# The second output projection of a two-layer backbone step by Strassen's scheme on quarters

## The chip, the cores and the metric

One core of a Trainium2 chip runs the whole step as one program. The metric is the device time of one execution in microseconds (us), the median of several runs. PE is the matrix engine, PEld its weight loads, DVE the vector engine, ACT the scalar engine, POOL GpSimd, SP the engine whose queue issues nearly all transfers (DMAs). Weights lie in HBM, work tiles in SBUF, matmul results in PSUM.

## The reference

Tokens are 512 latent and 128 context ones, T = 640 in all; the width is 2048. Cut to what matters here:

```python
def _odd_mixer(h, w_in, w_out, ...):
    xb, gate = jnp.split(h @ w_in, 2, axis=-1)
    ...                                   # conv, gates, two scans -> y
    return (y * jax.nn.silu(gate)) @ w_out, final

xp = xp + g_p * out_p                     # context tokens
xs = xs + g_s * out_s                     # latent tokens
y_prompt = _rmsnorm(xp, final_norm_g)
y_sample = _rmsnorm(xs, final_norm_g)
```

The change concerns the last `@ w_out` (2048 x 2048, the array `c_out`), the residual with its gate, and the final norm. All is float32.

## The kernel before, in words

Activations lie transposed: channel tile k (128 channels, k = 0 to 15) by 640 tokens. A float32 product is made of three matmuls in the type float32r: each operand is split into a high part and the rest, and high by high, high by low and low by high are added up in PSUM. For the weights ACT casts the high part (`wh`, 128 x 1024: eight 128 x 128 blocks, half of the weights of one output tile) and DVE subtracts it from the raw tile (`wl`). `Stream` does that: `load` issues the DMA of a raw tile, `advance` the cast, `finish` the subtraction and then the next load; there are 3 buffers each of `raw`, `wh` and `wl`.

`project` makes one output tile: for both token halves (320 each) and 16 k it issues three matmuls, 96 in all, into two PSUM accumulators from `r_acc` (three buffers). The second output projection is 16 such tiles. Tile 0 is made at the end of the stage before ("lru", the recurrent mixer), the others in the stage "out1". `mixd1` (profile name `mixe`) holds the mixer's output tiles in HBM; `load_mixed` brings them back while the last gate projection runs, and `split_mixed` makes their high and low parts (`mh`, `ml`; `md` for one that needs no trip).

After each tile `out_project` works on it: DVE adds the residual `xr` to the gated accumulator (`xo`), ACT squares it (`sq`), DVE sums the squares (`sqa`), ACT multiplies by the norm's weight. For the last two tiles the token halves are cut at 384 and `ending` closes the norm of the first 384 tokens while PE still works on the other 256: column sums of `sqa` by PE, a reciprocal root on 3 or 2 columns (`small`), a diagonal matrix `dg` spread by PE, 16 multiplications shared by DVE and POOL, and 8 DMAs of `y`.

The program is straight-line code. A planner writes it at build time: each piece of work is a Python generator, `Clock` keeps an estimated time per engine, and `Order` lets a piece go on when the estimate says that its data is ready. What it decides is the order of instructions on each engine. On the chip every engine runs its list strictly in that order, and so does each issuing queue: an instruction that waits holds up all behind it.

`Clock` puts every transfer on one line at 360 KB per us, whatever its kind:

```python
if op == "dma_start":
    self.t[engine] = at + (0.47 if engine == "Q" else 1.0)
    ...
    begin = max(at + 1.1, self.t["DMA"])
    end = self.t["DMA"] = begin + size / 360e3
```

## Time and profile before

| | |
|---|---|
| median of 3 runs | 2304.67 us (2299.78 to 2307.65) |
| the profiled execution | 2299.91 us, its span 2298.1 us |
| PE, PEld, DVE, ACT, POOL busy | 93%, 88%, 73%, 47%, 37% of the span |
| stage "out1" | from about 2066 us to the end |
| DMA in the steady part of out1 | about 100 GB/s |

Busy time of PE counts a matmul from its start to its modelled end, and neighbours overlap: a 128 x 320 matmul is shown with 0.31 us while a new one starts every 0.147 us. So PE's pace is read from the distance of starts, or from a queue that follows PE, not from the mean of one matmul. Starts in the timeline are us from the span's start. Where a group of rows ends in "12.3 <-PE acc", the engine stood idle for 12.3 us before those instructions and PE's `acc` ended the wait.

### The profile page before, as it was taken

Reading aid. Unit: us, or ns where it says so; the run is one execution under the profiler, and the core shown is the slowest. Engines: PE = TensorE matmul, PEld = TensorE weight load, DVE = VectorE, ACT = ScalarE, POOL = GpSimd, SP = SyncE. Lnnn points to the kernel's source line nnn. Section 1 sums busy time; section 2 is a strip of 40 time slices with the busy share of each in tenths; the row PEclk is TensorE's granted clock in tenths of the full one; section 3 lists DMA queues with packets and bytes.
Section 4 is the critical chain, followed back from the end, with each engine's and each line's share of the span. In section 5 each row is a group of like instructions: output and inputs, shape, how many; then the busy total and the mean of one; then the engine's idle time right before and its main releaser. Section 6 shows DMA issues by size and latency. Waiting matters only on the chain. (4 is left out here: it accounts for less than half of the span.)

```text
span 2298.1 us, 37534 instructions
## 1 busy us (share of the span) xinstructions
PE 2130.1 (93%) x14567; PEld 2025.0 (88%) x14567; DVE 1673.0 (73%) x2560; ACT 1086.3 (47%) x1814; POOL 845.3 (37%) x678
## 2 busy tenths in 40 slices
PE   4899989988989999999998999899999999999997
PEld 1579888877878999999987999799999999999997
DVE  6968775898877888887887676787886667783334
ACT  5555555555553333333353333576565554662222
POOL 3424443445344666566563222444530101110002
PEclk9899999999999999999998999999999999999998
DMA  9864434222225444444455555333322222243223
GB/s 367 301 247 131 136 114 135 84 100 86 93 95 194 140 147 147 140 139 146 148 200 175 191 188 183 98 116 114 117 79 88 85 85 86 80 171 109 97 97 131
DMA packets 127449, 320.62 MB, mean 140 GB/s; under 512 B 14246, under 2 KB 22279, under 8 KB 127272
## 3 DMA queue, kind: packets, MB, share of 16 engines
q1 hardware_dynamic: 125480, 313.20, 40.5%
q0 software_dynamic: 1792, 5.04, 0.7%
q8 instruction: 114, 1.87, 0.3%
q14 instruction: 63, 0.52, 0.1%
HBM read 281.86 MB, written 36.32 MB: 138 GB/s over the span
## 5 line engine op out<-in xcount | busy, mean ns | idle before, releaser
L318 PE MATMUL acc<-h,wh 128*128 128x320 f32 x2544 | 810.0, 318 | 24.9 <-DVE xo L318 9.0
L318 PE MATMUL acc<-h,wl 128*128 128x320 f32 x2544 | 793.0, 312 | 0.0
L318 PE MATMUL acc<-l,wh 128*128 128x320 f32 x2544 | 792.4, 311 | 0.0
L318 POOL TENSOR_TENSOR macc<-macc,mprod 128x512 f32<-128x512 f32 x289 | 434.7, 1504 | 559.2 <-ACT mprod L318 474.1
L318 PEld LDWEIGHTS acc<-h,wh 128*128 128x128 f32 x2544 | 485.2, 191 | 36.0 <-DVE xo L318 9.3
L318 PEld LDWEIGHTS acc<-l,wh 128*128 128x128 f32 x2544 | 484.7, 191 | 0.1
L318 PEld LDWEIGHTS acc<-h,wl 128*128 128x128 f32 x2544 | 483.6, 190 | 0.0
L318 ACT CAST wh<-raw 128x1024 fp32r<-128x1024 f32 x241 | 252.4, 1047 | 413.0 <-PE acc L318 370.0
L318 DVE TENSOR_TENSOR wl<-raw,wh 128x1024 fp32r<-128x1024 f32 x241 | 318.0, 1320 | 171.5 <-ACT wh L318 169.2
L318 PE MATMUL acc<-mh,wh 128*128 128x320 f32 (+2 forms) x1024 | 318.9, 311 | 11.2 <-ACT mh L318 8.8
L318 ACT ACTIVATE mprod<-mraw,vec 128x512 f32<-128x512 f32 x289 | 209.1, 724 | 237.6 <-POOL macc L318 169.5
L318 PE MATMUL acc<-mh,wl 128*128 128x320 f32 (+2 forms) x1024 | 318.3, 311 | 0.0
L318 PE MATMUL acc<-ml,wh 128*128 128x320 f32 (+2 forms) x928 | 288.0, 310 | 2.4 <-DVE ml L318 2.4
L318 DVE SCALAR_TENSOR_TENSOR macc<-mraw,vec,macc 128x512 f32<-128x512 f32 x191 | 186.2, 991 | 100.8 <-DMA mraw<-in_mod_w_dram 77.3
L318 PEld LDWEIGHTS acc<-mh,wh 128*128 128x128 f32 x1024 | 193.2, 189 | 14.6 <-ACT mh L318 9.2
L318 PEld LDWEIGHTS acc<-mh,wl 128*128 128x128 f32 x1024 | 193.6, 189 | 0.0
L318 PEld LDWEIGHTS acc<-ml,wh 128*128 128x128 f32 x928 | 175.1, 189 | 4.1 <-DVE ml L318 3.7
L318 POOL COPY stout<-hs 128x1 f32<-128x1 f32 x32 | 20.5, 639 | 319.2 <-DVE hs L318 319.2
L318 PE MATMUL g<-xhl,wh 128*128 128x322 f32 x512 | 115.7, 314 | 2.2 <-ACT ri L318 2.2
L318 POOL TENSOR_TENSOR y<-y,t 128x256 f32<-128x256 f32 x80 | 84.2, 1072 | 43.0 <-DVE t L318 34.1
L318 POOL TENSOR_TENSOR xo<-xo,sq 128x384 f32<-128x384 f32 (+1 forms) x13 | 11.5, 916 | 239.8 <-ACT sq L318 239.8
L318 DVE SCALAR_TENSOR_TENSOR xo<-acc,modc,xr 128x128 f32<-128x128 f32 (+3 forms) x96 | 38.8, 434 | 82.6 <-PE acc L318 73.7
(303 smaller groups left out, 3369.4 us busy)
## 6 DMA issues: line engine op xcount, KB each, us to landing
mraw<-in_mod_w_dram SPq DMA_DIRECT2D x256, 256.0 KB, 3.3
raw<-in_w_in_dram SPq DMA_DIRECT2D x95, 512.0 KB, 4.0
mraw<-in_mod_w_dram SPq DMA_DIRECT2D x64, 512.0 KB, 7.4
raw<-in_c_in_dram SPq DMA_DIRECT2D x64, 512.0 KB, 3.7
raw<-in_c_out_dram SPq DMA_DIRECT2D x34, 512.0 KB, 3.9
raw<-in_w_out_dram SPq DMA_DIRECT2D x32, 512.0 KB, 4.0
hd<-ef SPq DMA_DIRECT2D x48, 256.0 KB, 3.9
raw<-in_c_gates_dram SPq DMA_DIRECT2D x16, 512.0 KB, 3.5
```

Source lines behind the costliest of these rows:

```text
L318: f(*args, **kw)
```

## The change

The weight matrix W is cut into quarters W11, W12, W21, W22 (output half, then input half), the 2048 channels of the mixer's output into two halves, the tokens into FORE (0 to 319) and REAR (320 to 639). That gives four token quarters: b11 (channels 0 to 1023, FORE), b12 (the same channels, REAR), b21 and b22 (channels 1024 to 2047). One `quarter` is 8 k by 3 matmuls of 320 columns, 24 matmuls into one accumulator. Strassen's scheme, in Winograd's form, needs seven products of quarters where the plain way needs eight; each product has 8 output tiles. Two of the seven use plain weights (`PLAIN`: b11 with W11, b21 with W12), the other five use sums of quarters (`SUMS`: s2, s1, s3, w22, s4 for each output tile j; w22 is a plain weight, but multiplies a sum of tokens).

The sums of tokens (t1, t2, t3, t4) are made by `token_sum` on DVE, POOL and ACT in the first part of out1, from `mixe` tiles that are loaded once more; t3 and t4 go to HBM (`t34d`) and come back (`waiting`) when the tiles that hold b11 and b21 are free. The sums of weights are made by `Pairs`: SP loads a quarter tile of W21 into an SBUF place, and POOL's queue issues a DMA that adds a second one from HBM to it (`accum_op=ALU.add`). For each j there are three loads (W21 twice, W22), four adding DMAs, two sign changes on ACT, and the cast and subtraction for five items. There are six places of 512 KB (`cr`, three of them the old `raw` buffers); s4 is made in the place of s2. Four more PSUM buffers (`more`) are opened, and `bank` takes the free one that has been free for longest. `use` adds the products to the output tiles, `summed` does residual, squares and weight for a half tile of 320 tokens, `normed_out` the norm of FORE and of REAR.

```diff
+PLAIN = [(0, 0), (0, 1), (0, 2), (1, 0), (1, 1)] + [(_n, _j + 3 - _n) for _j in range(5) for _n in (0, 1)] + [(1, 7)]
+SUMS = [(_j, _s) for _j in range(7) for _s in ("s2", "s1", "s3", "w22", "s4")] \
+    + [(7, _s) for _s in ("s2", "s3", "w22", "s1", "s4")]
...
+    def add(self, t, j, q):
+        while self.clock.t["G"] > Ring.order.time:
+            yield 0.2
+        self.G.dma_start(out=t, in_=self.src[j][("w11", "w21", "w22", "w12").index(q)], accum_op=ALU.add)
+        yield
...
+    def sums(self):
+        for j in range(len(self.src)):
+            t = self.raw[j, "s1"] = yield from self.place()
+            self.Q.dma_start(out=t, in_=self.src[j][1])
+            u = self.raw[j, "s2"] = yield from self.place()
+            Ring.order.spawn(self.two(j, t, u))
+            yield 2.0
+            for name in ("s3", "w22"):
+                t = self.raw[j, name] = yield from self.place()
+                self.Q.dma_start(out=t, in_=self.src[j][1 if name == "s3" else 2])
...
+    def two(self, j, t, u):
+        yield
+        yield from self.add(t, j, "w22")
+        self.S.activation(u, t, AF.Identity, scale=-1.0)
+        self.there.add((j, "s1"))
+        yield
+        yield from self.add(u, j, "w11")
+        self.there.add((j, "s2"))
+
+    def three(self, j, t):
+        yield
+        self.S.activation(t, t, AF.Identity, scale=-1.0)
+        yield
+        yield from self.add(t, j, "w11")
+        self.there.add((j, "s3"))
...
+    def work(self, i):
...
+        self.S.copy(wh, t)
+        yield
+        self.V.tensor_sub(wl, t, wh.bitcast(F32))
+        if name == "s2":
+            Ring.order.spawn(self.four(j, t))
+        else:
+            self.places.free(t)
...
+            o = acc[:, 0:HT]
+            od.until(clock.ready([wh[:, k, :], wl[:, k, :], xh, xl], [o] if k == 0 else []))
+            for n, (w_, x) in enumerate(((wh, xh), (wh, xl), (wl, xh))):
+                PE.matmul(o, lhsT=w_[:, k, :], rhs=x, start=(k == n == 0), stop=(k == 7 and n == 2))
...
-        project(parts2, put_later(first_out), lambda k: od.drain(lambda: parts2[k] is not None))
+        for j in range(3):
+            sums_[j] = r_acc.get()
+            quarter(ws, "b11", sums_[j])
         od.drain()
...
+            S.copy(h22, b22)
+            yield
+            V.tensor_sub(l22, b22, h22.bitcast(F32))
+            V.tensor_sub(b22, b22, b12)
+            yield
+            G.tensor_sub(b12, b12, b11)
+            G.tensor_add(b11, b11, b22)
+            yield
+            S.activation(h2, b11, AF.Identity, scale=-1.0)
+            S.copy(h1, b12)
+            G.tensor_sub(b21, b21, b11)
+            yield
+            V.scalar_tensor_tensor(l2, b11, -1.0, h2.bitcast(F32), op0=ALU.mult, op1=ALU.subtract)
+            V.tensor_sub(l1, b12, h1.bitcast(F32))
...
+        def bank():
+            od.drain(lambda: r_acc.open() or r_more.open())
+            first = lambda r: min([r.over(i) for i, t in enumerate(r.held) if t is None], default=1e9)
+            owner = min((r_acc, r_more), key=first)
...
+            if name == "w12":
+                yield from add(j, "p1", (j, 0), c, acc, True, "c11", True)
+            elif name == "s2":
+                yield from add(j, "p1", a, c, acc, True, "u2", False)
+            elif name == "s3":
+                yield from add(j, "u2", b, a, acc, True, "u3", False)
+            elif name == "w22":
+                yield from add(j, "u3", c, b, acc, True, "c21", True)
+            elif name == "s1":
+                yield from add(j, "u3", a, a, acc, False, "u4", False)
+                yield from add(j, "c21", b, b, acc, True, "c22", True)
+            else:
+                yield from add(j, "u4", a, a, acc, True, "c12", True)
...
+        for n, j in PLAIN[3:]:
+            acc = bank()
+            quarter(ws, "b21" if n else "b11", acc, (lambda k: freed.add((n, k))) if j == 7 else None, pr)
+            od.spawn(use(j, "w12", acc) if n else plain_first(j, acc))
+        of = {"s2": "t2", "s1": "t1", "s3": "t3", "s4": "b22", "w22": "t4"}
+        for j, name in SUMS:
+            acc = bank()
+            quarter(pr, of[name], acc, None, pr)
+            od.spawn(use(j, name, acc))
         od.drain()
```

Three places in the order of instructions follow. The first is ACT's list in the steady part of out1. Before, one output tile gives two casts, a square and a weighting:

```order
L318 CAST wh_22740<-raw_22576 128x1024
L318 CAST wh_22798<-raw_22633 128x1024
L318 ACTIVATE sq_22812<-xo10_22677 128x640
L318 ACTIVATE xo10_22677<-xo10_22677,vec_74 128x640
L318 CAST wh_22859<-raw_22696 128x1024
```

In the change one turn of j (here from s2 of j = 6 to w22 of j = 6 and the sign change for s3 of j = 7) reads as follows; `cr_23249` is the place in which s1 of j = 7 is made, `cr_23055`, `cr_23182` and `cr_23214` hold s1, s3 and w22 of j = 6:

```order
L326 ACTIVATE cr_23282<-cr_23249 128x1024
L326 CAST wh_23325<-cr_23055 128x1024
L326 ACTIVATE sq_23343<-xo12_21567 128x320
L326 ACTIVATE xo12_21567<-xo12_21567,vec_74 128x320
L326 ACTIVATE sq_23358<-xo12_21567 128x320
L326 ACTIVATE xo12_21567<-xo12_21567,vec_74 128x320
L326 CAST wh_23370<-cr_23182 128x1024
L326 ACTIVATE sq_23395<-xo4_21563 128x320
L326 ACTIVATE xo4_21563<-xo4_21563,vec_74 128x320
L326 CAST wh_23412<-cr_23214 128x1024
L326 ACTIVATE cr_23376<-cr_23376 128x1024
```

The sign change that reads the sum of j = 7 (first row) now stands ahead of the cast for s1 of j = 6, whose matmuls come a whole turn sooner. The second place is POOL's list in the same stretch. Before, nothing stood there between the mixer's last `hs` and the final multiplications:

```order
L318 TENSOR_TENSOR hs_21198<-hs_21198,hs_21231 128x128
L318 TENSOR_TENSOR xo0_21600<-xo0_21600,sq1_21594 128x384
```

In the change the adding DMAs stand there, 32 in all, here those for s4 of j = 5, s2 and s3 of j = 6, s1 of j = 7, and s4 of j = 6:

```order
L326 DMA cr_22894<-in_c_out_dram 128x1024
L326 DMA cr_23088<-in_c_out_dram 128x1024
L326 DMA cr_23182<-in_c_out_dram 128x1024
L326 DMA cr_23249<-in_c_out_dram 128x1024
L326 DMA cr_23088<-in_c_out_dram 128x1024
```

The third is SP's list at the start of out1. Before, it alternates one residual and two weight tiles:

```order
L318 DMA out_new_s_dram<-stout 128x32
L318 DMA xr<-x1d 128x640 x2
L318 DMA raw<-in_c_out_dram 128x1024 x2
L318 DMA xr<-x1d 128x640
L318 DMA raw<-in_c_out_dram 128x1024 x2
```

In the change the tiles of the mixer are loaded again there, and the first stores of t3 and t4 follow:

```order
L326 DMA out_new_s_dram<-stout 128x32
L326 DMA cr<-in_c_out_dram 128x1024
L326 DMA xr<-x1d 128x320
L326 DMA xo_21561<-mixe_100 128x2x320
L326 DMA xo_21565<-mixe_108 128x2x320
L326 DMA xo_21562<-mixe_101 128x2x320
L326 DMA xo_21566<-mixe_109 128x2x320
L326 DMA raw<-in_c_out_dram 128x1024
L326 DMA xo_21563<-mixe_102 128x2x320
L326 DMA xo_21567<-mixe_110 128x2x320
L326 DMA cr<-in_c_out_dram 128x1024
```

So the weights of the plain products now queue behind the mixer's tiles on SP.

## Rows read from the trace of the kernel before

**Rows 1.** The page: engines over the span, and PE's granted clock in 40 slices.

```profile
PE 2130.1 (93%) x14567; PEld 2025.0 (88%) x14567; DVE 1673.0 (73%) x2560; ACT 1086.3 (47%) x1814; POOL 845.3 (37%) x678
PEclk9899999999999999999998999999999999999998
```

**Rows 2.** Stretches, from:to; us, busy PE PEld DVE ACT POOL, clock, DMA share, GB/s.

```profile
2050.00:2060.00 10.00, 9.00 (x62) 8.73 (x61) 9.34 (x18) 7.80 (x12) 0.00 (x0) 1.00 1.04 409
2085.00:2141.40 56.40, 56.40 (x386) 56.40 (x386) 17.63 (x25) 14.27 (x17) 0.00 (x0) 1.00 0.31 105
```

**Rows 3.** Timeline of SP's queue, steady part: start, us, what.

```profile
2107.12 0.42 SPq L318 DMA_DIRECT2D xr<-x1d  x1
2113.80 7.38 SPq L318 DMA_DIRECT2D raw<-in_c_out_dram  x2
2121.23 0.43 SPq L318 DMA_DIRECT2D xr<-x1d  x1
```

**Rows 4.** Timeline of PE at tile 0, the one wait there in brackets.

```profile
2059.55 0.41 PE L318 MATMUL acc<-ml,wh 128*128 128x320 f32 x1 [1.00 <-DVE ml L318]
```

**Rows 5.** DVE and ACT by shape, 2040 to 2298: busy us, mean ns, idle before.

```profile
L318 DVE TENSOR_TENSOR wl<-raw,wh 128x1024 fp32r<-128x1024 f32 x34 | 42.0, 1234 | 72.9 <-ACT wh L318 72.9
L318 DVE SCALAR_TENSOR_TENSOR xo<-acc,modc,xr 128x320 f32<-128x320 f32 x14 | 7.7, 551 | 45.2 <-PE acc L318 40.4 <-DMA xr<-x1d 4.7
L318 DVE SCALAR_TENSOR_TENSOR xo<-acc,modc,xr 128x128 f32<-128x128 f32 x18 | 6.0, 342 | 2.4 <-PE acc L318 2.4
L318 DVE SCALAR_TENSOR_TENSOR xo<-acc,modc,xr 128x192 f32<-128x192 f32 x14 | 5.8, 417 | 15.9 <-PE acc L318 15.9
L318 DVE TENSOR_TENSOR xo<-xo,acc 128x384 f32<-128x384 f32 x8 | 4.1, 546 | 0.7 <-ACT sq L318 0.7
L318 DVE TENSOR_TENSOR xo<-xo,acc 128x256 f32<-128x256 f32 x11 | 3.7, 412 | 1.8 <-ACT sq L318 1.8
...
L318 ACT CAST wh<-raw 128x1024 fp32r<-128x1024 f32 x34 | 35.7, 1050 | 152.2 <-PE acc L318 149.6 <-issue 2.6
...
L318 ACT ACTIVATE xo<-xo,vec 128x384 f32<-128x384 f32 x2 | 1.2, 618 | 0.1
L318 ACT ACTIVATE sq<-xo 128x384 f32<-128x384 f32 x2 | 1.0, 522 | 7.1 <-DVE xo L318 7.1
```

**Rows 6.** DMA issues: queue, count, KB each, median us to landing; over the span.

```profile
raw<-in_c_out_dram SPq DMA_DIRECT2D x34, 512.0 KB, 3.9
```

**Rows 7.** The same, 690 to 712 us, where the DMA engines are full.

```profile
sig<-in_sig_dram POOLq DMA_DIRECT2D x2, 768.0 KB, 8.3
raw<-in_w_in_dram SPq DMA_DIRECT2D x3, 512.0 KB, 8.2
```

**Rows 8.** The tile `invo`, 512 KB on POOL's queue: its landings.

```profile
DMA to landing us min/median/max: 8.5/10.7/12.9
```

**Rows 9.** Timeline of ACT, one cast in the steady part.

```profile
2111.46 1.05 ACT L318 CAST wh<-raw 128x1024 fp32r<-128x1024 f32 x1 [6.00 <-PE acc L318]
2112.42 0.73 ACT L318 ACTIVATE sq<-xo 128x640 f32<-128x640 f32 x1
```

**Rows 10.** POOL's multiplications at the end, by shape, columns as in group 5.

```profile
L318 POOL TENSOR_TENSOR xo<-xo,sq 128x256 f32<-128x256 f32 x5 | 3.5, 725 | 4.6 <-ACT sq L318 4.6
```

**Rows 11.** The chain that ended last, its end: start, us, what.

```profile
2272.17 9.98 PE acc L318 x80
...
2282.18 1.07 DVE xo L318 x3
...
2288.64 0.42 DVE xo L318
...
2289.39 2.98 DVE xo L318 x9
```

More of the change, by code (lines that the diff above doesn't have):

```diff
@@ L20 @@
 NS = 512
+HT = 320
 GZ = 642
@@ L450, in get, with __init__, empty, over @@
         return t
+class Places(Bank):
+    def __init__(self, stream, places, shape, dtype, name):
+        self.stream, self.places, self.shape, self.dtype, self.name = stream, places, shape, dtype, name
+        self.held = [None] * len(places)
+    def empty(self, i):
+        ws = self.stream
+        return self.held[i] is None and (
+            i >= RAWS or ws.loaded == len(ws.src) and all(n % RAWS != i for n in (*ws.raw, *ws.left))
+        )
+    def over(self, i):
+        p, tag = self.places[i]
+        return self.order.clock.over(p.used[tag][-1], "Q") if p.used.get(tag) else 0.0
+    def open(self, n=1):
+        return sum(self.empty(i) for i in range(len(self.held))) >= n
+    def ready(self, n=1):
+        return sum(self.empty(i) and self.over(i) <= self.order.time for i in range(len(self.held))) >= n
+    def get(self):
+        i = min((i for i in range(len(self.held)) if self.empty(i)), key=self.over)
+        p, tag = self.places[i]
+        t = self.held[i] = p.tile(self.shape, self.dtype, tag=tag, name=self.name, bufs=1)
+        return t
 class Stream:
@@ L2221, in _kernel, with out_project @@
         od.drain()
-    def out_project(op, layer, src, parts, first, keep, finish, xout, sqa, last=None):
-        r_x = Ring(op, [128, T], F32, "xr", 3 if last else 2)
+    def out_project(op, layer, src, parts, first, keep, finish, xout, sqa):
+        r_x = Ring(op, [128, T], F32, "xr", 2)
         r_sq = Ring(op, [128, T], F32, "sq", 1)
-        pairs = []
         def residual(i):
@@ L2264, in then @@
                 xout[i] = o
-            return putter(write, then) if i < 14 or last is None else last(i, write, o, pairs)
+            return putter(write, then)
         for i in range(16):
@@ new lines, in _kernel, with residuals, token_sums @@
+        finals = [x for j in range(8) for x in ((j, 0), (j + 8, 0), (j + 8, 1), (j, 1))]
+        def residuals():
+            for i, h in finals:
+                while not r_x.ready():
+                    yield 0.3
+                x = res[i, h] = r_x.get()
+                Q.dma_start(out=x, in_=x1d[i][:, REAR if h else FORE])
+                yield
+        def token_sums():
+            for k in range(8):
+                m, c = (k % 6, REAR) if k % 6 < 4 else (k % 4 + 2, FORE)
+                y = [pairs[m + 4 * d][:, :, c] for d in range(2)]
+                while not (
+                    k in mixed_done and k + 8 in mixed_done and (k < 6 or k - 6 in made) and clock.ready([mixd1[k], mixd1[k + 8]], y, "Q") <= od.time
+                ):
+                    yield 0.3
+                for d in range(2):
+                    Q.dma_start(out=y[d], in_=mixd1[k + 8 * d].rearrange("p (c t) -> p c t", c=2))
+                yield 0.5
+                od.spawn(token_sum(k, y))
@@ new lines, in _kernel, with waiting @@
+        made = []
+        def waiting(n):
+            for m in range(4):
+                for k in (2 * m, 2 * m + 1):
+                    while not (k in made and {(n, 2 * m), (n, 2 * m + 1)} <= freed and clock.ready([t34d[k]]) <= od.time):
+                        yield 0.3
+                    name = "t4" if n else "t3"
+                    hi, lo = quarter_at(name, k)
+                    Q.dma_start(out=lo.bitcast(F32), in_=t34d[k][:, FORE if n else REAR])
+                    od.spawn(split_waiting((name, k), hi, lo))
@@ new lines, in _kernel, with place, plain_first, add @@
+        owners = {}
+        def place(i, h):
+            return x2[i][:, REAR if h else FORE]
+        def plain_first(j, acc):
+            while j >= 4 and 4 + j // 6 not in made:
+                yield 0.3
+            S.copy(place(j + 8, 0), acc[:, 0:HT])
+            drop(acc)
+            yield
+            done.add((j, "p1"))
+        def add(j, needs, to, of, acc, last, tells, ends):
+            while (j, needs) not in done:
+                yield 0.2
+            V.tensor_add(place(*to), place(*of), acc[:, 0:HT])
+            if last:
+                drop(acc)
+            yield
+            done.add((j, tells))
+            if ends:
+                od.spawn(summed(*to))
```

296 lines of the change are left out of this document (216 added, 80 removed).

## The prediction

> **What bounds the kernel now.** I read the page first: PE is busy 93% of the span and its granted clock is nine tenths of full speed or more in all but three of 40 slices [rows 1]. Then the stretches of the last stage. There PE has no idle time, DVE works 18 us of 56 and ACT 14, and the DMA engines move about 105 GB/s where they reach 409 shortly before [rows 2]. So the projection runs at PE's pace, and everything else has room. That pace is read from SP's queue, which follows PE: residual tiles are asked for at 2107.12 and 2121.23, 14.11 us apart, and between them lie the 96 matmuls of one output tile [rows 3]. That is 0.147 us a matmul, 3.53 us for a quarter product of 24, and 17.64 us for the five products of one j. PE waits once, 1.0 us, at tile 0, for the low part of a mixer tile [rows 4]. After the last matmul the chain runs some 16 us over residual, squares, norm, multiplications and stores [rows 11].
>
> **PE's work.** Before: 16 tiles of 96, 1536 matmuls. After: seven products of eight tiles of 24, 1344. The matmuls keep their shape, so 192 go, at 0.147 us: **-28.2 us**, if PE stays the bound. At the start the first three products need only the first eight mixer tiles, and only their first 320 tokens, so the wait of 1.0 us should go: **-1.0**.
>
> **The other engines in the steady part.** Each turn of j is 17.64 us of PE. DVE has five subtractions of 1.23 us, six additions from PSUM (0.55 at 384 columns, 0.41 at 256, so 0.48 at 320), four half tiles of residual (0.55 in one piece or 0.42 + 0.34 in two) and four sums of squares, which I also take at 0.48: 6.2 + 2.9 + 2.6 + 1.9 = 13.6 us. ACT has five casts and two sign changes of the same size at 1.05 and four pairs of square and weighting, 0.52 and 0.62 at 384 columns, about 1.0 a pair at 320: 11.4 us [rows 5]. Both are below PE, at 77% and 65%. Before, they were at 31% and 25%; the cover is thinner, but no engine becomes the bound by its work alone.
>
> **The adding DMA.** No row shows one, so I call its time from issue on POOL to landing X and bound it. Below: a plain load of the same 512 KB, 3.9 us [rows 6]. Above: the slowest 512 KB on POOL's queue, `invo`, with 12.9 us, when the DMA engines were full and four others had been issued before it [rows 8]. Between them lies `sig`, 768 KB on the same queue, 8.3 us in the same crowd, where plain loads of 512 KB took 8.2 instead of 3.9 [rows 7]. The steady part won't be that full, but an addition has to fetch what it adds to, besides the 512 KB from HBM. I take **X = 6.5 us**, nearer to the plain load than to the crowd. The traffic of a turn, three loads, four additions and four residual halves, is 4.3 MB if an addition counts once, 245 GB/s.
>
> A rule of the Trainium skill speaks against the change here: "Collectives: The Full Stack", section "The bandwidth ceiling: the fold count and why AG ≠ RS ≠ AR", has an addition in the DMA engines read two sources, and so run at half the rate of a copy. By that rule a turn reads 6.4 MB, 364 GB/s, and an addition takes the DMA engines 2.6 us where a copy at 409 GB/s takes 1.3; on the plain load's 3.9 us, with 0.5 for the other queue, that makes an estimate of X = 5.7, and the sum below would be 2284. No row of before can show it.
>
> **Who waits for X.** The place of W22's quarter of j becomes free when it is cast and subtracted, and then takes the load of W21 for s1 of j + 2. POOL's queue adds W22, and ACT makes the sign change that starts s2. In ACT's list this sign change stands ahead of the cast of s1 of j + 1, so ACT stands still until X is over, and behind it stand that cast, three pairs of square and weighting, the cast of s3, and the cast of W22 of j + 1, which closes a ring. Its length: from the start of a cast to the load that it frees, 2111.46 to 2113.80, is 2.34 us [rows 3, 9]; the load 3.9; then X; the sign change, the cast of s1 and the cast of s3 at 0.96 each, which is the distance from a cast to the next instruction [rows 9]; three pairs, 3.0; handovers 0.4. That is 12.5 + X, against 17.64 of PE. Up to X = 5.1 the ring costs nothing. At 6.5 it is 19.0 us, 1.4 more than PE needs, in seven turns 9.5 us. The lead eats a part of that: an item is cast when its product is still two away, 7.05 us, of which 2.4 go to cast and subtraction, so about 4.3 us are spent before PE waits. The other two additions on that path (W11 for s2, W12 for s4) have more than 11 us each. Steady loss: **+5.2** (0 at X = 5.1 to 50 at X = 12.9).
>
> **Where plain products turn into sums.** Before the third product of sums, PE has 15 products, 53 us. In that time SP's queue must bring 8 weight halves (4.2 MB), 16 mixer tiles (5.2), 4 quarters for j = 0 and 1 (2.1), residuals (0.5), store t3 and t4 (2.6) and load t3 back (1.3), and POOL's queue makes four additions (2.1 to 4.2 MB): 18 to 20 MB, 44 to 49 us at 409 GB/s [rows 2]. So the DMA engines are 83 to 93% full where now they are at a quarter, and SP's list is strict: a store of t34d that waits for a sum of tokens holds up the weights behind it. POOL has 24 additions of 0.73 us at 256 columns [rows 10], some 22 us at 320, which fits. I charge one load as late as those in the full stretch, 8.2 instead of 3.9 [rows 6, 7]: **+4** (0 to 13, three of them).
>
> **The end.** Behind the last product stands one more addition from PSUM (0.48). The last half has 320 tokens and not 256: 11 multiplications on DVE at 0.48 instead of 0.41 [rows 5], +0.8; 0.5 MB more of `y` in the last stores at 409 GB/s, +1.3, half of it under the multiplications. DVE's list puts eight multiplications of FORE among the steps of REAR, 3.8 us, where before two stood there, 1.1; I count half of the difference. With 0.1 for the residual that makes 3.4, say **+4** (2 to 6).
>
> **Sum.** -28.2 - 1.0 + 5.2 + 4 + 4 = -16.0 us. Against the profiled execution's 2299.9 that is 2284; its time is the lowest of those shown, 4.8 under the median, so for a median I predict 2304.7 - 16 = **2289 us**.
>
> **Rivals.** (a) All hidden: X is 5 us or less and the queue keeps up. Then -28.2 - 1.0 + 4 = -25, **2279**. For it: a load in the steady part lands after 3.9 us. Against it: the ring leaves nothing over, and the traffic is more than twice today's. (b) The adding DMA becomes the bound and the kernel **slower**. With X at `invo`'s median of 10.7 us the ring is 23.2 us, 5.6 over PE, 39 in seven turns, less 4.3 of lead: -28.2 - 1.0 + 35 + 8 = +14, **2318**; at 12.9 us 2334. It decides from X = 8.8 us, where the ring gives back all that PE saves. For it: POOL's queue has shown 8.5 to 12.9 us for 512 KB; and if an addition took the engines three times a copy's 1.3 us, the four of a turn with the 2.2 MB of plain traffic would fill 21 us of 17.64 by themselves. Against it: that was in a crowd of six. (c) The start of the stage is short of DMA: three loads late, 13 us instead of 4, and ACT's casts behind late tiles hold up the weights' casts. Then -16 + 9 = -7, and with a little more from the same crowd for the first turns about **2300**, no measurable change.
>
> **Chances.** Runs of before lie within 0.35% of each other; 0.3%, 7 us, is about what can be told from no change. The forecast, X of 5.5 to 8 us with a start that costs up to 8, has 0.48 and its own range, 2280 to 2298. (a) 0.17, (b) 0.21, (c) 0.14. Faster: 0.46 of the forecast, all of (a), 0.04 of (c), 0.67. The same, 2298 to 2312: 0.02, 0.05 of (b), 0.09 of (c), 0.16. Slower: 0.16 of (b), 0.01 of (c), 0.17. The range runs from 2275, which holds nearly all of (a), to 2317, which leaves out half of (b): 2275 to 2317.
>
> **What would show it.** PE: starts still 0.147 us apart, 1344 matmuls in the projection. The additions: their landing in the DMA view, 5.5 to 8 us; under 5 is (a), over 8.8 is (b). ACT: in each turn one wait of the sign change for a DMA, some 4 to 6 us, ahead of a cast; PE's waits behind `wl`, about 1 us a turn, and none before the lead is spent, so none for j = 0 and 1. If PE waits for `wl` more than once a turn, or the wait stands at the cast of s2 or s4, the ring is not the one that I drew. At the start: PE waits for weights or token sums between the plain products and s3 of j = 0, about 4 us in all, and DMA near 400 GB/s there. At the end 18 to 22 us from the last matmul of a product to the last store. The prediction fails if the additions are far from 6.5 us, if DVE's list, 77% full and in strict order, holds up the subtractions (PE would wait for `wl` while ACT had cast long before), or if the sums of tokens arrive later than the plain products last.

## The result and the profile after

The changed kernel takes 2326.19 us, median of 6 runs (2324.07 to 2333.84), against 2305.54 of before beside it: ratio 1.0104, 95% interval 1.0089 to 1.012. It is **slower, by 21 us in the medians and 24 by the ratio**; 2289 with a range up to 2317 was predicted.

The page of the changed kernel, its engines and PE's granted clock, against [rows 1]:

```profile
span 2322.3 us, 37713 instructions
...
PE 2119.1 (91%) x14377; PEld 2009.0 (87%) x14377; DVE 1743.9 (75%) x2703; ACT 1141.2 (49%) x1928; POOL 903.6 (39%) x731
...
PEclk9899999999999999999989999899999999998998
```

PE has 190 recorded matmuls less, and only 11 us less busy time in a span that is 24 us longer: it waits, and its granted clock is below nine tenths in 5 slices instead of 3. Stretches of the changed kernel, columns as in [rows 2]: the junction from plain products to sums, then the sums.

```profile
2085.00:2141.40 56.40, 41.07 (x231) 39.03 (x231) 42.62 (x56) 26.97 (x51) 27.15 (x24) 0.83 0.91 283
2150.00:2250.00 100.00, 90.64 (x572) 87.62 (x571) 59.19 (x101) 50.41 (x71) 16.66 (x19) 0.95 0.90 205
```

In the same 56.4 us PE had 386 matmuls before and now has 231. The DMA engines, a third busy before, are at 0.9 to the end of the loads.

To put the loss into stages I read five starts from PE's timeline. The first is a **mark**, a matmul of a gate projection some 70 us ahead of the stage "out1"; the program up to there is the same. Rows of the changed kernel: the mark, the first product with `t2h` (that of s2, the first of the five of each j) of j = 0, 1 and 7, and the last product's end.

```profile
1996.71 0.45 PE L326 MATMUL g<-xhl,wh 128*128 128x322 f32 x2
...
2127.81 0.30 PE L326 MATMUL acc<-t2h,wh 128*128 128x320 f32 x1
...
2155.95 0.31 PE L326 MATMUL more<-t2h,wh 128*128 128x320 f32 x1
...
2281.10 0.31 PE L326 MATMUL acc<-t2h,wh 128*128 128x320 f32 x1
...
2299.80 0.31 PE L326 MATMUL more<-qh,wl 128*128 128x320 f32 x1
```

And of the kernel before, the mark and the last matmul:

```profile
1992.85 0.46 PE L318 MATMUL g<-xhl,wh 128*128 128x322 f32 x2
...
2281.86 0.28 PE L318 MATMUL acc<-mh,wl 128*128 128x256 f32 x1
```

From the mark to the span's end it was 2298.1 - 1992.85 = 305.2 us, of which 16.2 lie behind the last matmul. With 192 matmuls (28.2 us) less, 8 turns of 17.64 us for the sums and the same 16.2, the first product of sums would begin 305.2 - 28.2 - 141.1 - 16.2 = 119.7 us after the mark, or 118.7 without the wait at tile 0. Measured:

| stage | if PE were the bound | changed kernel | lost |
|---|---|---|---|
| mark to first product of sums | 118.7 | 131.1 | 12.4 |
| first turn (j = 0 to 1) | 17.6 | 28.1 | 10.5 |
| six turns (j = 1 to 7) | 105.8 | 125.2, 20.9 each in the mean | 19.4 |
| last j, to its last matmul | 17.6 | 18.7 | 1.1 |
| behind it, to the end | 16.2 | 22.5 | 6.3 |

That is 49.7 lost against 29.2 won, +20.5; mark to end 325.6 against 305.2. The last j takes 18.7 us in e4 and k1 below too, which have no adding DMA.

PE's one long wait in the first turn is for the low part of a token sum, t2, which DVE makes behind low parts of the sums that come back from HBM and of weights; DVE has no gap in the 10 us before. Here the changed kernel's, and that of f1 below, where no addition is made:

```profile
2136.36 0.63 PE L326 MATMUL acc<-t2l,wh 128*128 128x320 f32 x1 [5.41 <-DVE t2l L326]
```

```profile
2125.62 0.64 PE L326 MATMUL acc<-t2l,wh 128*128 128x320 f32 x1 [5.32 <-DVE t2l L326]
```

Where a steady turn goes, from three timelines of the changed kernel. SP's queue, two loads that each take the place of W22's quarter, one turn apart; then POOL's queue, with four adding DMAs; then ACT:

```profile
2186.53 0.33 SPq L326 DMA_DIRECT2D cr<-in_c_out_dram  x1
...
2208.15 0.33 SPq L326 DMA_DIRECT2D cr<-in_c_out_dram  x1
```

```profile
2188.19 0.88 POOL L326 DMA_DIRECT2D cr<-in_c_out_dram  x1 [8.17 <-ACT cr L326]
2192.36 0.88 POOL L326 DMA_DIRECT2D cr<-in_c_out_dram  x1 [3.29 <-DVE xo L326]
2193.40 0.88 POOL L326 DMA_DIRECT2D cr<-in_c_out_dram  x1 [0.17 <-issue]
2200.77 0.88 POOL L326 DMA_DIRECT2D cr<-in_c_out_dram  x1 [6.49 <-ACT cr L326]
```

```profile
2199.42 1.06 ACT L326 ACTIVATE cr<-cr 128x1024 f32<-128x1024 f32 x1 [8.68 <-DMA cr<-in_c_out_dram]
2200.38 1.03 ACT L326 CAST wh<-cr 128x1024 fp32r<-128x1024 f32 x1
...
2203.23 1.03 ACT L326 CAST wh<-cr 128x1024 fp32r<-128x1024 f32 x1
...
2205.59 1.03 ACT L326 CAST wh<-cr 128x1024 fp32r<-128x1024 f32 x1
```

This is the ring of the prediction, step by step. A load starts at 2186.53; the addition to it is issued at 2192.36, 5.8 us on (the view names a DVE instruction as what ended POOL's wait there); ACT's sign change has stood for 8.68 us when that lands, at 2199.42, 7.1 us on; then the casts of s1, s3 and W22 at 2205.59, and 2.6 us later the next load. 21.6 us, against 12.5 + 6.5 = 19.0: the load took 1.9 us more than its 3.9, the addition 0.6 more than its 6.5. The six turns lie between 19.5 and 23.8 us.

### The profile page after: what moved, and what is told of

The parts are those of the page before. It is cut to its first block, busy times and chain, and to the rows that moved or that the text cites. A ratio compares the mean times of both kernels' runs of the same rounds, so it can differ in the third digit from the quotient of the medians.

```text
span 2322.3 us, 37713 instructions
## 1 busy us (share of the span) xinstructions
PE 2119.1 (91%) x14377; PEld 2009.0 (87%) x14377; DVE 1743.9 (75%) x2703; ACT 1141.2 (49%) x1928; POOL 903.6 (39%) x731
## 5 line engine op out<-in xcount | busy, mean ns | idle before, releaser
L326 PE MATMUL acc<-h,wh 128*128 128x320 f32 x2544 | 810.9, 319 | 25.8 <-DVE xo L326 8.2
L326 DVE TENSOR_TENSOR wl<-raw,wh 128x1024 fp32r<-128x1024 f32 x223 | 299.5, 1343 | 111.3 <-ACT wh L326 108.8
L326 ACT CAST wh<-raw 128x1024 fp32r<-128x1024 f32 x223 | 233.4, 1047 | 279.0 <-PE acc L326 226.9
L326 PE MATMUL acc<-mh,wh 128*128 128x320 f32 x512 | 160.5, 313 | 17.4 <-ACT mh L326 13.9
L326 PE MATMUL acc<-mh,wl 128*128 128x320 f32 x512 | 159.6, 312 | 0.0
L326 POOL COPY stout<-hs 128x1 f32<-128x1 f32 x32 | 20.5, 640 | 319.2 <-DVE hs L326 319.2
L326 PE MATMUL acc<-ml,wh 128*128 128x320 f32 x448 | 138.9, 310 | 0.0
L326 PEld LDWEIGHTS acc<-mh,wh 128*128 128x128 f32 x512 | 97.0, 189 | 20.5 <-ACT mh L326 14.5
L326 PEld LDWEIGHTS acc<-mh,wl 128*128 128x128 f32 x512 | 97.3, 190 | 0.0
L326 PEld LDWEIGHTS g<-xhl,wh 128*128 128x128 f32 x512 | 87.0, 191 | 3.2 <-ACT ri L326 3.0
L326 POOL DMA_DIRECT2D cr<-in_c_out_dram x32 | 28.2, 921 | 155.4 <-ACT cr L326 79.3
L326 PEld LDWEIGHTS acc<-ml,wh 128*128 128x128 f32 x448 | 84.8, 189 | 0.0
```

The source lines that it names most:

```text
L326: f(*args, **kw)
```

## The experiments

The table gives the same five starts for every kernel: us from the mark to the first product of sums, the first turn, the mean of the six after it, the last matmul to the end, mark to end, and the ratio to the kernel before with its interval (or the one time). The mark itself lay between 1985.5 and 1997.2 us in these executions, so mark to end compares single profiles better than their times do. It is not exact either: for the kernels from e1 on with several runs, their median less their mark to end lies between 1990 and 1996 us, so a difference of some 3 us between two rows is not told from chance.

One part of it can be taken out. Right behind the mark the rest of the gate projection, the same 96 matmuls of `g` in all of them, took 17.9 to 18.0 us in the changed kernel, the one before, e1, e3, e4, e5, f2, k1 and k2, and 16.8 in the others, with a mean granted clock of 0.76 and 1.00 in the 7 us after its one wait of 2 us. Where rows of the two kinds are compared, 1.1 us are added below to the shorter kind.

| kernel | first sum | turn 1 | turns 2-7 | end | mark to end | ratio or us |
|---|---|---|---|---|---|---|
| changed kernel | 131.1 | 28.1 | 20.9 | 22.5 | 325.6 | 1.0104 |
| e1 | 133.1 | 32.7 | 19.4 | 21.6 | 321.6 | 1.0044 (1.0026-1.0062) |
| e2 | 139.3 | 20.8 | 19.5 | 22.4 | 318.0 | 1.0043 (1.0025-1.0061) |
| e3 | 129.6 | 25.8 | 17.8 | 22.4 | 303.3 | 2296.8 us |
| e4 | 119.7 | 24.3 | 17.6 | 22.8 | 291.2 | 2278.6 us |
| e5 | 126.5 | 21.6 | 23.3 | 22.3 | 328.9 | 2319.4 us |
| e6 | 140.8 | 20.0 | 23.1 | 22.6 | 340.4 | 1.0145 (1.0128-1.0163) |
| e7 | 118.7 | 22.0 | 21.8 | 22.5 | 312.9 | 1.0025 (1.0006-1.0044) |
| e8 | 125.1 | 27.8 | 22.8 | 22.4 | 330.6 | 1.0096 (1.0075-1.0117) |
| f1 | 123.0 | 25.3 | 17.6 | 22.5 | 295.2 | 2291.4 us |
| f2 | 128.7 | 24.2 | 26.5 | 22.3 | 353.0 | 1.0214 (1.0188-1.0241) |
| f3 | 122.7 | 27.3 | 20.9 | 22.4 | 316.4 | 1.0029 (1.0015-1.0044) |
| f4 | 139.4 | 21.4 | 20.2 | 22.1 | 322.9 | 2320.6 us |
| k1 | 128.9 | 24.8 | 17.6 | 22.3 | 300.4 | 0.9961 (0.9947-0.9976) |
| k2 | 129.3 | 27.5 | 18.0 | 22.3 | 305.9 | 0.9985 (0.9973-0.9998) |
| k3 | 127.9 | 24.7 | 17.6 | 21.8 | 298.8 | 0.9956 (0.9939-0.9973) |
| k4 | 122.6 | 21.8 | 17.7 | 21.9 | 291.4 | 0.9936 (0.9919-0.9952) |

### The steady turns: order (A) or full DMA engines (B)

**e1**, the planner books an adding DMA at twice its bytes (in `note`):

```diff
-            size = max(1, out.shape[0]) * self.size(out) * 4
+            size = max(1, out.shape[0]) * self.size(out) * (8 if kw.get("accum_op") is not None else 4)
```

> One number of the planner is changed: it books an adding DMA with twice its bytes, so that it reckons the sums ready later, and ACT's list comes out with the sign change for the sum of j+2 behind the casts of s1 and s3 of j+1 instead of ahead of them. The bytes, the DMAs and the matmuls stay. Theory A (the order ring): in the changed kernel ACT stands at the sign change, which waits for a load (5.8 to 6.0 us) and an adding DMA (6.3) in series, with the casts that TensorE needs behind it; a steady turn is then 21.25 us where the matmuls need 17.64. With the sign change behind the casts the ring is open: steady turn at most 18.5 us, and the total 2303 to 2312 us (2326 less some 7 turns of 2 to 3 us). Theory B (the DMA engines are full): their busy share is 0.89 over the steady turns, 18.9 us of each 21.25, and no order makes it less; the turn stays 20.5 or more and the total 2320 to 2328 us.

**e2**, the same with a seventh place:

```diff
-        spread = op.tile([128, HT], F32, name="spread")
+        spread = dg
...
-            Places(ws, [(wpool, f"raw{i}") for i in range(RAWS)] + [(op, f"cr{i}") for i in range(3)], [128, 8, 128], F32, "cr"),
+            Places(ws, [(wpool, f"raw{i}") for i in range(RAWS)] + [(op, f"cr{i}") for i in range(4)], [128, 8, 128], F32, "cr"),
```

> As the kernel in which the planner books adding DMAs at twice their bytes, and with seven places for the sums of weights instead of six (the seventh takes the room of the tile named spread, which shares dg's). Theory A (order ring): a place more lets the loads of j+2 start one product earlier, so the load and the add in series are covered; steady turn 17.6 to 18.2 us, total 2298 to 2308 us. Theory B (DMA engines full): more places only queue more bytes at the same engines; turn 20.5 or more, total 2318 to 2328 us.

Turns of 19.4 and 19.5 us: neither theory's number, though e1's 2311.9 us lies at the end of A's range; e2's 2312.5 lies between the two. The order, in e2 with a seventh place, gave back 1.4 to 1.5 us of 3.3. In e2 the DMA engines were busy for 92.4 of 100 us (57.3 for POOL's queue, 35.1 for SP's, 2150 to 2250), 18.0 us of a turn of 19.5, which is itself more than PE's 17.64: by that share, an estimate, the transfers alone would hold a turn above PE. What was won in the turns of e2 went partly back before the first sum, 139.3 us.

**e3**, POOL's DMAs overwrite instead of adding (the additions are left out):

```diff
-        self.G.dma_start(out=t, in_=..., accum_op=ALU.add)
+        self.G.dma_start(out=t, in_=...)
```

> The POOL DMAs of the sums overwrite instead of adding, so the sums of weights are left out (each tile holds the last quarter alone); bytes read from DRAM, number of DMAs, waits and ACT's order stay as in the changed kernel. What is left is the price of adding. Both theories: landing of the POOL DMA falls from 6.3 to 4 to 5 us, of the SP loads from 5.8 to 4 to 5 us, DMA busy share in the steady turns from 0.89 to 0.55 to 0.65. Theory A (order ring): 12.5 + (4.5 - 3.9) + 4.5 = 17.6 to 18.5 us a turn. Theory B (engines full): 17.64, PE-bound. Total 2296 to 2306 us by both. If the junction (2066 to 2140) still loses 16 us, its loss is not that of the adds; if the total is below 2300, it is.

Landings on the page of e3, POOL's queue and SP's:

```profile
cr<-in_c_out_dram POOLq DMA_DIRECT2D x32, 512.0 KB, 4.8
cr<-in_c_out_dram SPq DMA_DIRECT2D x24, 512.0 KB, 5.0
```

The ring by the prediction's formula is then 12.5 + (5.0 - 3.9) + 4.8 = 18.4 us. The turns were 17.6 three times, by my reading while the lead lasted, and then 18.0, 17.9 and 18.1: the formula is right to 0.4 us here, with the landings put in that were measured. The time before the first sum hardly moved, and first sum and first turn together still lose 19.1 us of 22.9. The total under 2300, which was to show that the junction's loss is that of the adds, came from the turns.

**f2**, the adding DMAs are made, but the planner books nothing for them:

```diff
-        self.G.dma_start(out=t, in_=..., accum_op=ALU.add)
+        self.G.engine.dma_start(out=t, in_=..., accum_op=ALU.add)
```

> The reverse: the adding DMAs are issued, but the planner books nothing for them, so that ACT's order is that of the kernel without POOL DMAs. Theory O: the first product of sums begins at 119 to 122 us, as there; theory D: at 127 us or more. In the steady part the planner now takes the sums to be ready at once, so the sign changes stand at least as early as in the changed kernel: by the ring 21 us a turn or more, total 2320 to 2335 us; by the DMA engines alone 20 to 21 us, 2318 to 2326 us.

Order matters more than I gave it. A turn takes 26.5 us, with the same transfers, and now the DMA engines have room. The stretch 2150 to 2250 of f2, with DMA share 0.71:

```profile
2150.00:2250.00 100.00, 79.09 (x451) 76.12 (x450) 44.48 (x76) 38.63 (x55) 12.23 (x14) 0.83 0.71 167
```

In this order the first sign change stands one cast earlier, ahead of that of s2 of j + 1, and the other one ahead of the cast of W22, so the ring holds a cast and a sign change more and ACT waits up to 11.3 us at its first step. 19.4, 20.9 and 26.5 us a turn come from the same transfers in three orders. The engines alone can't give that; the ring was named, and the total, 2348 us, is 13 above its range. The planner's bookings move other instructions too, so the one place in ACT's list is not tried by itself.

**f4**, e2 with one more DMA per j that nobody waits for and the planner does not book:

```diff
+            if j > 1:
+                self.Q.engine.dma_start(out=self.spare[j], in_=self.src[j][0])
```

> The kernel with seven places and adds booked twice, and per j from 2 on one DMA more on SP that copies 512 KB from DRAM to a spare tile in DRAM, that nobody waits for and the planner does not book: the order is unchanged, the DMA engines get more to do. Theory B (what is left above 17.64 us in that kernel, whose turns two to seven take 19.5 us in the mean, is the DMA engines being full): the turns that have loads left grow by 1.5 to 3 us, 21 to 22.5 in the mean of turns two to five (now 21.1 in the mean of its first four), total 5 to 15 us more. Theory A (it is order that is left): less than 0.5 us a turn.

Mark to end grew by 4.9 us over six such DMAs, 6.8 in the last turn alone (17.9 to 24.7) while turns two to six did not grow. That is less than B expected and more than A, and little more than the 3 us that are not told from chance. So with the order open the DMA engines are a limit near by, whose share of the remaining 1.8 us I can't separate from order.

### The junction

**e4**, no POOL DMAs at all, and **f1**, booked but not issued (the additions are left out in both):

```diff
-        self.G.dma_start(out=t, in_=..., accum_op=ALU.add)
+        self.clock.note("G", "dma_start", (), dict(out=t, in_=..., accum_op=ALU.add))   # f1 only
```

> The 32 POOL DMAs of the sums are left out altogether (the sums of weights are not made), all else stays. Steady turn 17.64 us by all theories (load 3.9 to 4.5 us and sign change only). What it tells apart is the junction: if the stretch 2066 to 2140 loses its 16 us by the DMA engines, which the adds, the mixer tiles and the remaining plain loads fill together (busy share 0.97 to 1.00 in 2080 to 2120), then less than 8 us are lost here and the total is 2280 to 2292 us; if it loses them by the planner's order and by the trip of the token sums through DRAM (landing median 8.1 us), 12 us or more stay lost and the total is 2293 to 2303 us.

> The adding DMAs are booked by the planner as before but not issued (the additions are left out); TensorE, ACT, VectorE and SP then have the changed kernel's order word for word, only POOL loses its 32 DMAs. In the kernel that leaves them out of the booking too, the first product of sums began 119.7 us after the last 322-column product of the projections before (in the changed kernel 131.1), and the turns after it were 24.3 and then 17.6. Theory O (order: the planner, which books adds, puts instructions that wait ahead of casts in the junction): 127 us or more to the first product of sums here. Theory D (the adds' transfers fill the DMA engines): 119 to 122 us. The steady turns say nothing here (no add to wait for): 17.6 by both.

Without adds a turn is 17.6 us, so the PE term holds. Before the first sum, e4 loses 1.0 us, f1, with the changed kernel's order, 5.4 (4.3 and the 1.1 of the mark), and the changed kernel 12.4: the order costs 4.4 and the adds 7.0. f1 came out 1 us above D's range, 2 with the 1.1, and 3 to 4 below O's; e4's one time, 2278.6, is 1.4 below the range of full DMA engines, with a mark 11 us ahead of the changed kernel's. The first turn stays 7 to 8 us too long without any add, with the wait for `t2l` shown above (2.4 us in e4).

**e7** and **f3**, the four adds of j = 0 left out, unbooked and booked:

```diff
+        if j > 0:
-        self.G.dma_start(out=t, in_=..., accum_op=ALU.add)
+            self.G.dma_start(out=t, in_=..., accum_op=ALU.add)
+        else:
+            self.clock.note("G", "dma_start", (), dict(out=t, in_=..., accum_op=ALU.add))   # f3 only
```

> The changed kernel without the four adding DMAs of j=0 (their additions are left out), which all fall between 2075 and 2131; those of j=1 to 7 stay. Theory D (the DMA engines are full in the junction, and the adds fill them): 2066 to 2140 loses 6 to 9 us instead of 15, as in the kernel without any POOL DMA (5.6), the steady turns stay at 21.2 us, total 2314 to 2319 us. Theory T (the trip to t34d and the copy that waits for it): 13 us or more stay lost, total 2322 to 2328 us.

> Only the four adds of j=0 are booked and not issued (left out); order as in the changed kernel but for two rows. Leaving them out of the booking too brought the first product of sums from 131.1 to 118.7 us and the total 18 us down. Theory O: first product of sums at 127 us or more, total 2320 to 2326 us. Theory D: 118 to 121 us, total 2306 to 2312 us.

Those four cost 7.3 us before the first sum with the order kept (f3: 122.7 and the 1.1), 11.3 with their places in the order too (e7: 118.7 and the 1.1). f3's total, 2307.8, lies in D's range; e7's, 2307.1, lies 7 us under D's and more under T's. So the adds being there make the larger part of the loss. That full DMA engines are the reason is not shown: an add that is left out takes its bytes with it and also the wait for its landing. At a copy's price (e3) 129.6 us were needed, only 1.5 less, though the engines' share from 2085 us to the first sum fell from 0.89 to 0.79. Part of this is the clock: from the end of `g` to the first sum PE stood for 9.5 us in the changed kernel, 6.4 in e3, 4.9 in f1, but in e3 more of the rest ran at the lower clock. The three, length less PE's busy time, columns as in [rows 2]:

```profile
2014.60:2127.80 113.20, 103.72 (x674) 102.53 (x674) 83.49 (x121) 61.99 (x101) 38.52 (x35) 0.94 0.69 223
```

```profile
2009.80:2121.40 111.60, 105.22 (x674) 104.04 (x673) 84.15 (x122) 62.01 (x100) 37.72 (x36) 0.94 0.66 226
```

```profile
2011.20:2117.30 106.10, 101.25 (x674) 100.20 (x673) 83.20 (x121) 61.63 (x100) 36.26 (x32) 0.98 0.67 223
```

**e5**, the trip of the token sums through DRAM left out:

```diff
-            Q.dma_start(out=t34d[k].rearrange("p (c t) -> p c t", c=2), in_=y[1])
...
-                    Q.dma_start(out=lo.bitcast(F32), in_=t34d[k][:, FORE if n else REAR])
+                    Q.dma_start(out=lo.bitcast(F32), in_=mixd1[k + 8][:, FORE if n else REAR])
```

> The trip of the two token sums through DRAM is left out of the changed kernel: no store to t34d, and the products with w22 and s1 take their tokens from the mixer's tiles in DRAM (so these products have other numbers). The adding DMAs, ACT's order and the 16 half loads stay. Theory T (the trip): the junction (2066 to 2140) loses its 17 us because ACT's copy of a plain product into a pair tile waits 13.4 us for the store out of that tile, with the casts of the next weights queued behind the copy; without the store less than 9 us are lost there and the total is 2312 to 2318 us. Theory D (the DMA engines are full there): the copy only stands where the next late transfer would have stopped the engines; at least 12 us stay lost and the total is 2320 us or more.

The wait at which I aimed, in ACT's timeline of the changed kernel, its longest in the junction:

```profile
2116.91 0.75 ACT L326 COPY xo<-acc 128x320 f32<-128x320 f32 x2 [13.39 <-DMA t34d<-xo]
```

Without the store this copy no longer waits, and the first sum of j = 0 comes 4.6 us and that of j = 1 11.1 us sooner. But mark to end is 328.9, no better: the planner's order changed with the edit, and the turns behind grew to 23.3. The one time of 2319.4 looks like a gain, but its mark lay 8 us early. T is right about the wait, and its total (2312 to 2318) did not come.

**e6**, the sums of weights held back; **e8**, POOL's part of the token sums on DVE:

```diff
+        while self.hold():            # e6: pr.hold = lambda: len(made) < 6
+            yield 0.3
...
-            G.tensor_sub(b12, b12, b11)      # e8, and so for the two others
+            V.tensor_sub(b12, b12, b11)
```

> One line holds back all loads and adding DMAs of the sums of weights until the token sums of six of the eight tiles are booked; everything moved is the same work later. Theory D (in the junction the DMA engines are full): 2066 to 2140 loses 8 to 12 us instead of 17, since the mixer's tiles no longer share the engines with four to eight adds; the steady turns stay at 21.2 us, total 2317 to 2322 us. Theory T (the copy that waits for the store to t34d): 15 us or more stay lost, total 2324 to 2330 us. If the first sums then come too late, the loss only moves to 2130 to 2160.

> The three operations of each token sum that POOL makes (24 of 128x320, mean 1.15 and 1.5 us in 2066 to 2140) are made by VectorE; nothing else changes. A third theory on the junction, C: VectorE and POOL slow each other there (wl takes 1.43 us beside POOL's sums instead of 1.22, ql<-xo,qh 0.78 instead of 0.47, t2l 0.82 instead of 0.48), so the sums of tokens come late by that; without it the junction loses 9 to 12 us instead of 15 and the total is 2320 to 2323 us. Theory D (DMA engines full): the sums were waiting for bytes anyway, 14 us or more stay lost, total 2324 to 2328 us.

e6 only moved the loss: PE stood for 18 us before the first sum, and 2334.8 us is above both ranges. e8 brought the first sum to 125.1, and lost it again in turns of 22.8; its ratio is that of the changed kernel, and its 2324.7 us lies in D's range. e5 to e8 also reorder the turns behind, which is why I take the junction's shares from f1 and f3, with e4 for what is left without adds.

### A version without adding DMAs

**k1**: four plain loads per j, and the four sums on DVE. **k2**: s1 and s4 on POOL instead. **k3**: k1, and POOL takes 10 of the first half's 16 last multiplications. **k4**: k3 with all token sums on DVE, as in e8. The remarks behind `#` are no part of the code.

```diff
+            w21 = yield from self.get(j, "w21")      # place() and a load on SP
+            w22 = self.raw[j, "w22"] = yield from self.get(j, "w22")
+            w11 = yield from self.get(j, "w11")
+            t = yield from self.place()
...
+        self.V.tensor_add(t, w21, w22)               # s1; self.G in k2
+        self.V.tensor_sub(w21, w11, w21)             # s3
+        self.V.tensor_sub(w11, w11, t)               # s2
...
+        self.V.tensor_add(self.raw[j, "s4"], self.raw[j, "s4"], t)   # s4, t is s2; self.G in k2
...
-                if k % 3 == 2:                       # k3 and k4
+                if k % 3 == 2 or not h and k % 3 == 1:
```

> The sums of weights are made by VectorE in SBUF instead of by adding DMAs: per j four plain loads (w21, w22, w11, w12) on SP, no POOL DMA and no sign change on ACT, four 128x1024 additions or subtractions on VectorE (1.1 to 1.3 us each, as the subtraction for wl 1.22 us). VectorE: 11 us a turn and 4.9 more, 16 of 17.64; DMA as in the kernel without POOL DMAs and one load more, busy share 0.35 to 0.45. Both theories A and B: turn 17.64 and 2280 to 2290 us, faster than the kernel before by 0.5 to 0.8%. A rival: VectorE at 90% in a strict order delays wl and the evictions, turn 18 to 18.5, 2288 to 2296 us.

> As the kernel with the sums on VectorE, but s1 and s4 on POOL (128x1024, 2.6 to 2.9 us by POOL's 725 ns for 128x256) and s2 and s3 on VectorE. VectorE 13.4 of 17.64 us a turn, POOL 5.6. If POOL and VectorE ran beside each other freely this is the lightest split: 2280 to 2286 us. Rival: both work in SBUF at the same time and slow each other (the subtraction for wl grows from 1.2 towards 1.9 us), and s1, on which s2 waits, comes 1.5 us later: 2286 to 2294 us, no better than the sums on VectorE alone.

> The kernel with the sums of weights on VectorE, and in the last normalisation of the first half POOL takes 10 of the 16 multiplications instead of 5. VectorE did 11 of them (0.4 us each) between the last products' additions, in the chain that ends the program (last matmul to the end: 22 us, before 16). If that chain is bound by VectorE the end shortens by 4 to 5 times 0.4 us: 2288 to 2290 us against 2291. Rival: POOL's ten (0.93 us each) slow VectorE beside them and end too late for the second half's share, so that nothing is gained: 2291 to 2294 us.

> As the kernel with the sums of weights on VectorE and the other split of the last multiplications, and the token sums' three POOL operations on VectorE too. In that kernel VectorE is busy for 19.9 of 20 us in 2100 to 2140, with wl at 1.9 us and the 128x320 operations at 1.15 us beside POOL instead of 1.22 and 0.48. Theory C: 24 operations of 0.48 us cost VectorE 11.5 us and give back 24 times about 0.68, 16 us, and each token sum is ready sooner: the junction loses 7 to 9 us instead of 11.6, total 2285 to 2288 us. Theory D (DMA engines): no change, 2288 to 2292 us.

k1 is faster than before by 0.39%. Its 2291.3 us lies in its rival's 2288 to 2296, but not for the rival's reason, turns of 18 to 18.5: the turns are PE's, and first sum and first turn lose 17.4 us, against 22.9 with the adds. k2 is slower than k1, as its rival said, and 3 us above the rival's range. k3 can't be told from k1; the end shrank by 0.5 us where 1.6 to 2 were hoped for, so the multiplications between the additions are at most a small part of those 6 us. **k4 is the best kernel of the study: 2287.44 us against 2301.16, faster by 0.64%** (0.48 to 0.81). DVE by shape in 2066 to 2140, busy us and mean ns, k1 and then k4:

```profile
L326 DVE TENSOR_TENSOR wl<-raw,wh 128x1024 fp32r<-128x1024 f32 x12 | 15.9, 1335 | 9.2 <-ACT wh L326 9.2
L326 DVE TENSOR_TENSOR ql<-xo,qh 128x320 fp32r<-128x320 f32 x16 | 12.0, 752 | 3.6 <-ACT qh L326 3.6
```

```profile
L326 DVE TENSOR_TENSOR wl<-raw,wh 128x1024 fp32r<-128x1024 f32 x11 | 13.3, 1220 | 7.1 <-ACT wh L326 7.1
...
L326 DVE TENSOR_TENSOR ql<-xo,qh 128x320 fp32r<-128x320 f32 x16 | 7.7, 484 | 2.3 <-ACT qh L326 2.3
```

With POOL out of the way the same DVE instructions are shorter, and k4 comes out 4.7 us under k3, in theory C's range, where e8 gained nothing. Whether it is the shorter instructions of DVE or the sums that no longer take POOL's 1.0 to 1.5 us each was not tried apart. The stretch 2150 to 2250 of k4 shows PE without a gap, DVE at 97%, DMA at 0.45:

```profile
2150.00:2250.00 100.00, 100.00 (x683) 100.00 (x683) 97.00 (x149) 52.51 (x77) 0.00 (x0) 1.00 0.45 144
```

## Why the prediction was wrong

**PE's work, -28.2, and the start, -1.0: right.** Turns are 17.6 us wherever nothing waits (e4, f1, k1), e4 needs 119.7 us to the first sum against 118.7, and the wait at tile 0 is gone: from 2010 us on PE first stands for more than 0.3 us at 2090.8 in the changed kernel.

**X = 6.5: right,** 6.3 in the median. DMA issues of the changed kernel, 2150 to 2250, median us to landing last, and its queues, POOL's first, with packets, MB and share of the 16 engines' time:

```profile
q0 software_dynamic: 2869, 10.44, 59.3%
q1 hardware_dynamic: 4562, 9.92, 30.1%
...
cr<-in_c_out_dram POOLq DMA_DIRECT2D x19, 512.0 KB, 6.3
cr<-in_c_out_dram SPq DMA_DIRECT2D x14, 512.0 KB, 5.7
```

Per MB an added byte takes the engines 59.3 / 10.44 = 5.7 us, a plain one 3.0: 1.9 times as long. (On POOL's own queue a copied byte took 2.8 in e3, 31.3% for 11.03 MB.) The rule of the Trainium skill that the prediction cites ("Collectives: The Full Stack", "The bandwidth ceiling: the fold count and why AG ≠ RS ≠ AR"), two reads and half the rate, agrees with these rows; its estimate of X = 5.7 was 0.6 short. What the prediction did not sum is the engines' time for a turn: at these measured prices 2.1 MB added and 2.2 plain are 18.6 us, over PE's 17.64.

**The steady turns, +5.2: mis-sized, measured +19.4** (six turns; the last j adds the 1.1 that it loses without adds too). The ring is the one drawn, with the wait at the step named, though of 6.1 to 9.5 us from the third turn on and not 4 to 6; 12.5 was wrong. It holds the load at 3.9 us [rows 6], a row of a kernel whose DMA engines were a third busy; beside the adds it takes 5.7 to 6.0. So the ring is 21.6 us and not 19.0, 1.9 of it by the load: I counted in X what the adds take for themselves, and nothing for what they take from the loads. That the price of a turn hangs on the order is shown by e1, e2 and f2; that the busy DMA engines are a limit close below it is an estimate from e2's shares, 18.0 us.

**The lead of 4.3 us: no help.** It was to pay for the first turns, but none of the turns behind the first was under 19.5 us; that the junction had already spent it is my reading.

**The junction, +4: the step that failed most, measured +22.9** (12.4 before the first sum, 10.5 in the first turn). I summed the bytes to 83 to 93% of the DMA engines, which came true (0.91), and then charged one late load. What is late is a store: t34d's, with ACT's copy of a plain product behind it for 13.4 us, and behind that the casts of the next weights. By f1 against the changed kernel the adds are 7.0 us of the first 12.4 and their places in the order 4.4 more. Of the 10.5 in the first turn 7 to 8 are there without any add (e4, f1). The wait in it is the one for `t2l`, 5.4 us in the changed kernel and 5.3 in f1, and the granted clock is 0.80 in the first 17 us of that turn. So a sign that the prediction gave for its failing came true, token sums that come later than the plain products last, and its other one, DVE's strict list that holds PE up, for `t2l` and not for `wl`; its sum had no term for either. What would bring `t2l` sooner wasn't tried apart; without the trip (e5) PE waits for it 0.8 us.

**The end, +4: measured +6.3**, just over its 2 to 6, and much the same in every kernel that sums on quarters (21.6 to 22.8 us). k3 shows that it isn't mainly DVE's multiplications; the rest stays open.

Rival (b) named the right sign and nearly the time (2318), by a wrong price, X = 10.7 where 6.3 was measured, so that its time came near is luck; (c) named the right place, with 13 us for it instead of 23. That both partly held together was not among my cases.

## What to carry to other kernels

When a change adds transfers, the landing times of the old loads are prices of the old traffic: raise them together with the new ones before a ring is summed. An instruction that waits for a load and an addition in series belongs behind the casts that don't need it; the planner that sets the order must know the true price, since the same transfers cost 19.4 to 26.5 us a turn in three orders. And where VectorE has room, four additions of 1.2 us in SBUF can be cheaper than four adding DMAs: 0.9961 against 1.0104 of the time before, here.

## What the runs showed of the hardware beyond that

An adding DMA is dearer to issue as well. POOL's issues of the changed kernel and of e3, mean ns behind the busy time:

```profile
L326 POOL DMA_DIRECT2D cr<-in_c_out_dram x32 | 28.2, 921 | 155.4 <-ACT cr L326 79.3 <-DMA xo<-mixe 30.0 <-DVE wl L326 15.0
```

```profile
L326 POOL DMA_DIRECT2D cr<-in_c_out_dram x32 | 17.4, 543 | 145.6 <-ACT cr L326 81.9 <-DMA xo<-mixe 30.7 <-DVE xo L326 14.6
```

PE's waits cost twice: in 2085 to 2141.4 PE is idle for 15.3 us, but its granted clock is 0.83 in the mean there, where it was 1.00 before [rows 2], so that 231 matmuls stand where 386 stood, and not the 281 that 41.07 of 56.4 us would hold at the full clock. The steady turns pay too: in 2150 to 2250 PE is idle for 9.4 us at 0.95 and does 572 matmuls, where k4 does 683 without a gap at 1.00. And the same program part up to the mark ended up to 11.6 us apart between executions, more than most effects in the second table: single times of such a kernel are read from a mark on.
